# A recurrence with decaying weights: shared PSUM banks, sums tile by tile, k rounded by its load, quarter tiles, and an order written by a list schedule

## The chip, the cores and the metric

The kernel runs on one core of a Trainium2 chip. The metric is the device time of one execution in microseconds (us). A core has five engines that run side by side: PE (TensorE, the matrix engine, which writes into PSUM), DVE (VectorE), ACT (ScalarE), POOL (GpSimd) and SP (SyncE, used here to issue DMAs). Each has its own queue of instructions and works through it in the order in which the program was written; between engines, semaphores say when data is ready. DMAs are issued by SP and by POOL, and by ACT once. PSUM has eight banks of 512 f32 columns.

## The reference

For each of 16 batches and 256 channels a pair (aa, bb) runs through 2048 time steps; pp is the logarithm of a common scale that keeps the exponentials in range. All tensors are f32, k and v are 16 x 2048 x 256.

```
for t in range(seq_len):
    ww = u + k[t];  qq = max(pp, ww)
    e1, e2 = exp(pp - qq), exp(ww - qq)
    output[t] = (e1*aa + e2*v[t]) / (e1*bb + e2 + 1e-08)
    ww = pp - w + k[t];  qq = max(ww, k[t])
    e1, e2 = exp(ww - qq), exp(k[t] - qq)
    aa, bb, pp = e1*aa + e2*v[t], e1*bb + e2, qq
```

Without the scale this is: the output is (a + exp(u+k) v) / (b + exp(u+k)), and then a becomes exp(k-w) a + exp(k) v, and b becomes exp(k-w) b + exp(k). So the weight with which a step counts later is the exponential of a running sum of k and w.

## The kernel before

Time is cut into 16 chunks of 128 steps, a chunk into two halves of 64. A tile n holds chunk n // 4 and four batches: 128 partitions (steps) by 1024 columns (four batches by 256 channels, or two groups i of 512 columns). There are 64 tiles. Per tile:

- `load_k`, `load_v` (lines 61 to 69) bring k and v, 0.5 MB each. `round_k` (L166, DVE) copies k into a tile `km` of type float32r, which the f32 matmuls read.
- `logs` (L183, L187, PE) builds the exponents in the PSUM tile `X`, 128 x 2 x 2 x 512 f32, four banks: for each kind q (q = 0: weight in the running sum, q = 1: weight of the step's own output) and each column group one matmul with one or two rows (positions times w, and u), and one 128 x 128 matmul with k (the running sums inside a half).
- `exps` (L193, L195, ACT) writes their exponentials in bf16 to places 0 and 1 of the ring `EZR`, which has twelve tiles. The first `HALVES` = 9 tiles take their banks in turn from `X` and from the bank pair that later holds denominators, in two instructions; the later ones take one instruction for both kinds.
- `cast_v` (L199) makes v bf16 in `vb`, of which there is one buffer; on DVE for the first eleven tiles, then on POOL. `times_v` (L204, DVE) writes the products of places 0 and 1 with v to places 2 and 3.
- `den` (L321, PE) and `num` (L335, PE) multiply the triangular matrix `L` and the identity `Id` (scaled in `LN`, `IdN`) with places 0, 1 and 2, 3, four matmuls of 128 x 128 by 512 columns each. Both matrices are zero between the two halves of 64. `recip` (L327, L328, ACT) makes 1/den as exp(-ln(den)); `mult` (L340, DVE) writes num/den and L341 stores it on SP's queue.

The state between halves runs through a small chain, once per chunk: `sums` (L231, 32 matmuls over the chunk's four tiles, column by column of tiles), `copy_sums` (L239), `turn` (L246), `copy_turn` (L252), `state_logs` (L256, ACT), `state_shift` (L261, POOL), `state_frames` (L266, a scan on DVE), `state_offsets` (L270 to L274, POOL), `state_weights` (L277, ACT), `state_chain` (L281, L284, DVE), `state_spread` (L289), `turn_back` (L300, PE), and `inject` (L305 and four small DMAs, L310), which writes the incoming states over the last row of each half in `EZR`. Only then can the chunk's den and num run. The PSUM tiles of `sums`, `turn`, `turn_back` and `num` share one pair of banks (`psn`, tag `num`), and `den` has a pair of its own (`psd`).

The order is written by hand: one loop over slots n (line 370). In slot n the exponentials of tile n are taken, the logs of tile n+1, the denominators and numerators of tile n-10 (`LAG` = 10), and at fixed places the pieces of the chain for the chunk that ended one to four slots before, from the table at line 346. Loads up to tile 15 are issued by SP and later ones by POOL, each in the slot after which a buffer comes free (`NBUF` = 7 for k and for v).

Of the kernel before, what the change touches and what calls it, by code (L numbers as in the profile page):

```python
# [7 lines left out]
F32 = mybir.dt.float32  # L8
# [7 lines left out]
def kernel(  # L16
# [13 lines left out]
    HS = 64  # L30
# [6 lines left out]
    FIRST = 16  # L37
    HALVES = 9
    NBUF = 7
    RS = 2.0 ** -20  # L40
    CAP = 54.0
    BIG = 1e30

    consts = ctx.enter_context(tc.tile_pool(name="consts", bufs=1))
    kpool = ctx.enter_context(tc.tile_pool(name="kpool", bufs=NBUF))
    vpool = ctx.enter_context(tc.tile_pool(name="vpool", bufs=NBUF))
    vbpool = ctx.enter_context(tc.tile_pool(name="vbpool", bufs=1))
    rpool = ctx.enter_context(tc.tile_pool(name="rpool", bufs=2))
    opool = ctx.enter_context(tc.tile_pool(name="opool", bufs=3))
    small = ctx.enter_context(tc.tile_pool(name="small", bufs=2))  # L50
    psx = ctx.enter_context(tc.tile_pool(name="psx", bufs=1, space=bass.MemoryType.PSUM))
    psd = ctx.enter_context(tc.tile_pool(name="psd", bufs=1, space=bass.MemoryType.PSUM))
    psn = ctx.enter_context(tc.tile_pool(name="psn", bufs=1, space=bass.MemoryType.PSUM))

    kr_of, vr_of, VB = {}, {}, {}

    def rows_of(x, n):
        c, p = divmod(n, 4)
        return x[4 * p:4 * p + 4, c * TC:(c + 1) * TC, :].rearrange("n t d -> t n d")

    def load_k(n, q):
        kr = kpool.tile([128, 4, Dm], F32, tag="kr", name="kr")
        K(q.dma_start(out=kr, in_=rows_of(k, n)))  # L63
        kr_of[n] = kr

    def load_v(n, q):
        vr = vpool.tile([128, 4, Dm], F32, tag="vr", name="vr")
        K(q.dma_start(out=vr, in_=rows_of(v, n)))  # L68
        vr_of[n] = vr


    wuf = consts.tile([128, 2, Dm], F32, tag="wuf", name="wuf")

    def rows_wu(q, x, g0):
        q = K(q.dma_start(out=wuf[g0::32, :, :], in_=bass.AP(
            tensor=x.tensor, offset=x.offset, ap=[[0, (128 - g0 + 31) // 32], [0, 2], list(x.ap[0])])))

    rows_wu(SC, w, 0)
    load_k(0, SP)
    rows_wu(SP, u, 65)  # L80
    load_k(1, SP)
    for n in range(NBUF - 1):
        load_v(n, SP)
        if n + 2 < NBUF:
            load_k(n + 2, SP)
    K(SC.preload_act_table_set("natural_log_exp_and_others"))
    Z = consts.tile([128, D], BF16, tag="Z", name="Z")
    K(DVE.memset(Z, 0.0))
    M1 = consts.tile([128, 128], F32, tag="M1", name="M1")
    I1 = consts.tile([128, 128], F32, tag="I1", name="I1")  # L90
    K(DVE.memset(M1, -1.0))
    K(DVE.memset(I1, 0.0))
    idle = psn.tile([128, 2, D], F32, tag="num", name="idle")
    for j in range(10):
        K(PE.matmul(idle[:, j % 2, :], Z[:, 0:128], Z, start=True, stop=True, skip_group_check=True))
# [12 lines left out]

    select(M1, GE, 0.0, -1, -1, [[1, 128]])
# [7 lines left out]

# [6 lines left out]
    WU = consts.tile([128, D], F32R, tag="WU", name="WU")  # L124
    for g, r in ((0, 1), (32, 1), (64, 2), (96, 2)):
        K(DVE.tensor_copy(WU[g:g + r, :], wuf[g:g + r].rearrange("p n d -> p (n d)")))

    mats = {}

    def sum_matrices():  # L130
        OH = consts.tile([128, 56], BF16, tag="OH", name="OH")
        fill(OH, 0.0)
        for h in range(2):
            fill(OH[HS * h:HS * h + HS, 22 + h:23 + h], 1.0)
            fill(OH[HS * h:HS * h + 1, 30 + h:31 + h], 1.0)
        Sel = consts.tile([128, 3, 2, 2, 4, 2], F32, tag="Sel", name="Sel")
        fill(Sel, 0.0)
        for j, r in ((0, 64), (1, 0), (2, 8)):
            for h in range(2):
# [32 lines left out]
    def part_of(n, q):  # L172
        if n >= HALVES:
            return X[:, q]
# [264 lines left out]
```

## Time and profile before

| | |
|---|---|
| three runs | 367.5, 367.6, 369.11 us, median 367.6 |
| profiled execution, from first to last instruction | 365.5 us; its time outside the span is not given, the median lies 2.1 above |
| busy: PE, DVE, ACT, POOL | 304.1, 257.4, 257.6, 196.3 us |
| granted TensorE clock, mean | 0.844 |
| DMA | 101.52 MB, mean 278 GB/s |
| chain that ended last | PE 62%, DVE 20%, POOL 6%, ACT 5% |

The profile is one execution. "Busy" is the time in which at least one instruction of the engine ran; since matmuls are pipelined, a busy PE can hold shorter work than it shows, so PE is better read from one group's start to the next group's start. The granted clock is the share of the full TensorE clock that the chip allowed at that moment. The chain of waits is followed back from the last instruction: at each step to what released it, or to the instruction before it on the same engine. A group's line gives: line of the kernel, engine, operation, output and inputs, shapes, count, busy us and mean ns of one, and then the idle time of the engine just before and what ended it.

### The profile page before, as it was taken

Reading aid. Unit: us, or ns where it says so; the run is one execution under the profiler, and the core shown is the slowest. Engines: PE = TensorE matmul, PEld = TensorE weight load, DVE = VectorE, ACT = ScalarE, POOL = GpSimd, SP = SyncE. Lnnn points to the kernel's source line nnn. Section 1 sums busy time; section 2 is a strip of 40 time slices with the busy share of each in tenths; the row PEclk is TensorE's granted clock in tenths of the full one; section 3 lists DMA queues with packets and bytes.
Section 4 is the critical chain, followed back from the end, with each engine's and each line's share of the span. In section 5 each row is a group of like instructions: output and inputs, shape, how many; then the busy total and the mean of one; then the engine's idle time right before and its main releaser. Section 6 shows DMA issues by size and latency. Waiting matters only on the chain.

```text
span 365.5 us, 4884 instructions
## 1 busy us (share of the span) xinstructions
PE 304.1 (83%) x1674; PEld 143.6 (39%) x1674; DVE 257.4 (70%) x355; ACT 257.6 (70%) x234; POOL 196.3 (54%) x279
## 2 busy tenths in 40 slices
PE   7789797969799696987989697988969788976682
PEld 2335353535344243443435253444425343533230
DVE  4773867878857757588866887575686889883652
ACT  1553558879758677679768797576775789993782
POOL 2700457887837738477764677575465745250100
PEclk9556658999859679699958997695887999998997
DMA  7999998899998979989998999889797995242465
GB/s 222 354 348 348 351 341 254 281 372 300 355 314 246 316 238 319 298 255 318 336 318 256 344 315 352 284 275 296 257 317 244 324 308 177 77 159 95 143 223 179
DMA packets 67498, 101.52 MB, mean 278 GB/s; under 512 B 5894, under 2 KB 55186, under 8 KB 67474
## 3 DMA queue, kind: packets, MB, share of 16 engines
q0 software_dynamic: 14080, 50.40, 43.2%
q1 hardware_dynamic: 53382, 50.80, 42.2%
q8 instruction: 13, 0.21, 0.2%
q14 instruction: 11, 0.09, 0.1%
q10 hardware_dynamic: 12, 0.01, 0.0%
HBM read 67.12 MB, written 33.55 MB: 275 GB/s over the span
## 4 chain that ended last, share of the span: by engine, by line
PE 62%; DVE 20%; POOL 6%; ACT 5%; issue 3%; DMA 2%; SPq 0%; DVEq 0%; POOLq 0%; ACTq 0%
PE X L187 17%; PE num L335 15%; PE den L321 13%; PE X L183 7%; DVE ot L340 7%; PE tot L231 6%; DVE km L166 4%; DVE EZR L204 4%; ACT rd L327 3%; PE TS L246 2%; PE CT L300 2%; DVE AB L284 2%; DMA vr<-in_v_dram 2%; ACT EZR L193 2%; POOL U L271 2%
## 5 line engine op out<-in xcount | busy, mean ns | idle before, releaser
L195 ACT ACTIVATE EZR<-X 128x2048 bf16<-128x2048 f32 x55 | 102.7, 1868 | 32.3 <-PE X L187 32.3
L340 DVE TENSOR_TENSOR ot<-num,rd 128x1024 f32<-128x1024 f32 x64 | 78.2, 1222 | 30.5 <-ACT rd L327 10.5
L199 POOL CAST vb<-vr 128x1024 bf16<-128x1024 f32 x53 | 55.0, 1038 | 83.1 <-DVE EZR L204 83.1
L204 DVE TENSOR_TENSOR EZR<-EZR,vb 128x2048 bf16<-128x2048 bf16 x64 | 79.5, 1241 | 2.1 <-ACT EZR L193 1.9
L327 ACT ACTIVATE rd<-den 128x1024 f32<-128x1024 f32 x64 | 65.1, 1017 | 16.6 <-PE den L321 13.9
L328 ACT ACTIVATE rd<-rd 128x1024 f32<-128x1024 f32 x64 | 67.8, 1059 | 2.0
L321 PE MATMUL den<-EZR,L 128*128 128x512 bf16 x128 | 42.4, 416 | 22.6 <-ACT rd L327 22.2
L166 DVE CAST km<-kr 128x1024 fp32r<-128x1024 f32 x64 | 55.5, 867 | 2.4 <-PE X L187 1.9
L187 PE MATMUL X<-km,NLE 128*128 128x512 f32 x128 | 54.1, 508 | 1.8 <-DVE km L166 0.9
L183 PE MATMUL X<-WU,CO 1*128 1x512 f32 (+1 forms) x256 | 42.8, 563 | 10.0 <-ACT EZR L195 5.8
L335 PE MATMUL num<-EZR,LN 128*128 128x512 bf16 x128 | 41.9, 412 | 8.7 <-DVE cb L305 5.7
L187 PE MATMUL X<-km,NLZ 128*128 128x512 f32 x128 | 47.8, 459 | 0.0
L68 POOL DMA_DIRECT2D vr<-in_v_dram x48 | 40.0, 832 | 5.0 <-DVE vb L199 4.2
L321 PE MATMUL den<-EZR,Id 128*128 128x512 bf16 x128 | 41.4, 407 | 0.0
L335 PE MATMUL num<-EZR,IdN 128*128 128x512 bf16 x128 | 41.3, 406 | 0.0
L63 POOL DMA_DIRECT2D kr<-in_k_dram x48 | 39.9, 830 | 0.0
L183 PEld LDWEIGHTS X<-WU,CO 1*128 1x128 f32 (+1 forms) x256 | 15.9, 205 | 47.2 <-issue 16.6
L193 ACT ACTIVATE EZR<-X 128x1024 bf16<-128x1024 f32 x18 | 17.9, 1022 | 20.2 <-PE X L187 20.1
L187 PEld LDWEIGHTS X<-km,NLZ 128*128 128x128 f32 x128 | 27.1, 219 | 9.2 <-issue 3.4
L187 PEld LDWEIGHTS X<-km,NLE 128*128 128x128 f32 x128 | 22.0, 215 | 20.3 <-issue 16.1
L239 DVE COPY ts<-tot 128x256 f32<-128x256 f32 x16 | 6.8, 425 | 32.2 <-PE tot L231 32.2
L231 PE MATMUL tot<-EZR,OH 128*32 128x256 bf16 x512 | 25.3, 364 | 1.4 <-DVE ot L340 1.4
(60 smaller groups left out, 233.3 us busy)
## 6 DMA issues: line engine op xcount, KB each, us to landing
out_dram<-ot SPq DMA_DIRECT2D x64, 512.0 KB, 5.4
kr<-in_k_dram POOLq DMA_DIRECT2D x48, 512.0 KB, 6.2
vr<-in_v_dram POOLq DMA_DIRECT2D x48, 512.0 KB, 7.3
kr<-in_k_dram SPq DMA_DIRECT2D x16, 512.0 KB, 8.8
vr<-in_v_dram SPq DMA_DIRECT2D x16, 512.0 KB, 8.7
EZR<-cb SPq DMA_DIRECT2D x56, 8.0 KB, 4.6
EZR<-cb POOLq DMA_DIRECT2D x8, 8.0 KB, 5.0
wuf<-in_w_dram ACTq DMA_DIRECT2D x1, 8.0 KB
```

The source lines that it names most:

```text
L166: K(DVE.tensor_copy(km, kr_of.pop(n)))
L183: K(PE.matmul(part_of(n, q)[:, i, :], CO[g:g + 1 + q, :], WU[g:g + 1 + q, :], start=True, stop=False, tile_position=(g, 0), skip_group_che ...
L187: K(PE.matmul(part_of(n, q)[:, i, :], (NLE, NLZ)[q], km[:, i, :], start=False, stop=True, skip_group_check=True))
L195: K(SC.activation(ez(n)[:, 0:2], X, ACT.Exp))
L199: K(eng.tensor_copy(vb, vr_of.pop(n)))
L204: K(DVE.tensor_mul(ez(n)[:, 2:4], ez(n)[:, 0:2], vb.unsqueeze(1).broadcast_to([128, 2, 2, D])))
L231: K(PE.matmul(t[32 * j:32 * j + 32, :], mats["OH"][:, s:s + 32], ez(4 * c + p)[:, 2 * q, i, 256 * x:256 * x + 256], start=p == 0 and x == ...
L321: K(PE.matmul(d[:, i, :], mats[m], ez(n)[:, q, i, :], start=q == 0, stop=q == 1, skip_group_check=True))
L327: K(SC.activation(rd, DEN.pop(n), ACT.Ln, scale=RS))
L328: K(SC.activation(rd, rd, ACT.Exp, scale=-1.0))
L335: K(PE.matmul(d[:, i, :], mats[m], ez(n)[:, q, i, :], start=q == 2, stop=q == 3, skip_group_check=True))
L340: K(DVE.tensor_mul(o.rearrange("p (i n) d -> p i (n d)", i=2), NUM.pop(n), RD.pop(n)))
```

## The change

- k is loaded directly into float32r tiles by POOL's DMAs, from tile 4 on; for the first four tiles SP loads it and DVE rounds it (`round_k`). w and u are loaded as float32r too. Loads from tile 4 on are POOL's.
- `X` is now two pairs of banks, given out to whoever comes next: logs of kind 0, logs of kind 1, or denominators. Logs and exponentials are two steps per tile, one per kind. `num` keeps a pair, `sums` has one bank of its own, and `turn`, `turn_back` share one.
- `sums` runs after each tile (8 matmuls) instead of once per chunk (32).
- `den` and `num` use 64 x 64 matmuls, eight per tile and kind, each in a quarter of the array; for the second column group the two halves of 64 steps land swapped, and `store` writes the output with three DMAs: one for two batches, two for the swapped halves of the others.
- The small POOL operations of the chain move to DVE. `vb` has two buffers, k and v eight.
- The order comes from a list schedule run while the program is built: each step has an engine, an assumed cost, what it follows, a due time and a buffer that it takes and gives back; the step that can start first is written next, and among those of one engine within 0.2 us the one due first. The assumed time of a tile is 3.9 us, the rates of the loads 0.35 and later 0.40 MB per us.

```diff
-    psx = ... psd = ... psn = ...
+    psx, psn, pst, pss = ...
     def load_k(n):
+        if n < BYSP:
+            KR[n] = vpool.tile([128, 4, Dm], F32, tag="vr", name="kf")
+            K(SP.dma_start(out=KR[n], in_=rows_of(k, n)))
+        else:
+            KR[n] = kpool.tile([128, 4, Dm], F32R, tag="kr", name="kr")
+            K(POOL.dma_start(out=KR[n], in_=rows_of(k, n)))
...
+    def logs(n, q, a):
+        km = KR[n].rearrange("p (i n) d -> p i (n d)", i=2)
+        for i in range(2):
+            g = 32 * (2 * q + i)
+            K(PE.matmul(X[:, a, i, :], CO[g:g + 1 + q, :], WU[g:g + 1 + q].rearrange("p n d -> p (n d)"),
+                        start=True, stop=False, tile_position=(g, 0), skip_group_check=True))
+        for i in range(2):
+            K(PE.matmul(X[:, a, i, :], (NLE, NLZ)[q], km[:, i, :], start=False, stop=True, skip_group_check=True))
-            K(SC.activation(ez(n)[:, 0:2], X, ACT.Exp))
+    def exps(n, q, a):
+        K(SC.activation(ez(n)[:, q], X[:, a], ACT.Exp))
...
+    def sums(n):
+        c, p = divmod(n, 4)
...
-        K(POOL.tensor_tensor(U[:, FR, :, 1:3], U[:, L1, :, 0:2], U[:, L1, :, 1:3], ALU.add))
+        K(DVE.tensor_tensor(U[:, FR, :, 1:3], U[:, L1, :, 0:2], U[:, L1, :, 1:3], ALU.add))
...
-                K(PE.matmul(d[:, i, :], mats[m], ez(n)[:, q, i, :], start=q == 0, stop=q == 1,
-                            skip_group_check=True))
+    def apply(out_tile, n, names, q0):
+        for s in range(2):
+            for i in range(2):
+                for h in range(2):
+                    r, o = HS * h, HS * ((h + i) % 2)
+                    K(PE.matmul(out_tile[o:o + HS, i, :], mats[names[s]][r:r + HS, r:r + HS],
+                                ez(n)[r:r + HS, q0 + s, i, :], start=s == 0, stop=s == 1,
+                                tile_position=(r, o), skip_group_check=True))
+    def den(n, a):
+        apply(X[:, a], n, ("L", "Id"), 0)
+    def num(n):
+        NUM[n] = psn.tile([128, 2, D], F32, tag="num", name="num")
+        apply(NUM[n], n, ("LN", "IdN"), 2)
...
+    def store(n):
+        c, p = divmod(n, 4)
+        o = OT.pop(n)
+        K(SP.dma_start(out=out[4 * p:4 * p + 2, c * TC:(c + 1) * TC, :].rearrange("n t d -> t n d"), in_=o[:, 0:2, :]))
+        for h in range(2):
+            t0 = c * TC + HS * (1 - h)
+            K(SP.dma_start(out=out[4 * p + 2:4 * p + 4, t0:t0 + HS, :].rearrange("n t d -> t n d"),
+                           in_=o[HS * h:HS * h + HS, 2:4, :]))
...
-    for n in range(NP + LAG + 2):
...
+            step(("LK", n), q, qc, load_k, (n,), behind=[("LK", n - 1)], due=t - 14 * SLOT, take=("V", -1 - n) if early else ("K", n), move=0.524)
+            step(("X", j, n), "ACT", 0.94, exps, (n, j), [("L", j, n), ("NUM", n - RING), ("S", n - RING)],
+                 [("X", 1 - j, n - 1 + j)], t, give=[("X", (j, n))])
+        step(("DEN", n), "PE", 0.55, den, (n,), [("IN", c)], [("DEN", n - 1)], t + e, take=("X", ("d", n)))
+        step(("LN", n), "ACT", 0.95, log_den, (n,), [("DEN", n)], [("INV", n - 1)], t + e, take=("RD", n),
+             give=[("X", ("d", n))])
+        step(("ST", n), "SP", 1.6, store, (n,), [("MUL", n)], due=t + e + 4, move=0.524)
...
+        pick = []
+        for eng, some in best.items():
+            t0 = min(some, key=lambda x: x[0])[0]
+            pick.append(min((x for x in some if x[0] <= t0 + 0.2), key=lambda x: x[1]))
+        t, _, name = min(pick, key=lambda x: x[:2])
```

## The prediction

> **What bounds the kernel now.** I read the table by stage first. The stages are cut at the first exponential (9.10 us), at that of tile 16 (80.86) and at that of tile 63 (322.79); the fifth row is the end of the steady stage, the last one a short dense stretch. Columns: length, busy time of PE, PEld, DVE, ACT and POOL with their instructions, granted clock, DMA share, GB/s.
>
> ```profile
> 0.00:9.10 9.10, 6.91 (x20) 2.52 (x20) 4.07 (x14) 1.29 (x2) 1.87 (x10) 1.00 0.72 221
> 9.10:80.86 71.76, 61.96 (x292) 29.56 (x292) 51.99 (x81) 44.28 (x43) 38.36 (x63) 0.71 1.03 330
> 80.86:322.79 241.93, 209.13 (x1231) 100.76 (x1231) 180.14 (x236) 186.47 (x166) 151.21 (x198) 0.87 0.88 285
> 322.79:365.50 42.71, 26.12 (x135) 10.79 (x133) 21.23 (x27) 25.59 (x27) 4.84 (x10) 0.91 0.48 162
> 292.61:322.79 30.18, 27.05 (x191) 13.85 (x191) 26.12 (x36) 27.68 (x26) 12.34 (x18) 1.00 0.55 181
> 160.00:167.00 7.00, 4.40 (x21) 1.83 (x18) 5.80 (x9) 5.07 (x6) 6.24 (x10) 1.00 1.04 383
> ```
>
> In the steady stage 47 tiles take 241.93 us, 5.15 each, and no engine is full: PE 86%, at a granted clock of 0.87, ACT 77%, DVE 74%, DMA 0.88. In the fifth row, with the clock at 1.00 and the loads over, the same order needs 30.18/7 = 4.31 us. So about 0.84 us per tile is lost to the clock and the transfers. Where, the chain of waits shows (start, length, what):
>
> ```profile
> 181.08 1.20 POOL U L271
> 182.28 0.07 issue
> 182.36 0.44 POOL U L272
> 182.79 0.02 issue
> 182.82 0.37 ACT G L277
> 183.18 0.92 ACT rd L327
> 184.10 0.04 issue
> 184.14 1.88 PE den L321 x4
> 186.02 0.61 PE CT L300 x4
> 186.63 0.02 issue
> 186.66 0.30 DVE cb L305
> 186.96 0.04 issue
> 187.00 1.87 PE num L335 x4
> 188.87 0.73 PE X L183 x2
> 189.59 2.00 PE X L187 x4
> ```
>
> The small chain of each chunk stands in the fixed order: ACT waits for POOL before L277, then PE for ACT, and PE is idle from 182.58 to 184.14. Then the clock falls to 0.50 (until 193.6): four den matmuls take 1.88 us instead of 0.86, four L187 2.00 instead of 1.12. What the operations cost, in groups:
>
> ```profile
> L195 ACT ACTIVATE EZR<-X 128x2048 bf16<-128x2048 f32 x55 | 102.7, 1868 | 32.3 <-PE X L187 32.3
> L199 POOL CAST vb<-vr 128x1024 bf16<-128x1024 f32 x53 | 55.0, 1038 | 83.1 <-DVE EZR L204 83.1
> L166 DVE CAST km<-kr 128x1024 fp32r<-128x1024 f32 x64 | 55.5, 867 | 2.4 <-PE X L187 1.9
> ```
>
> **The change, part by part**, per tile at full clock unless said.
>
> *ACT.* The exponential over 2048 columns becomes two over 1024. Back to back, three such take 2.90 us, 0.967 each, so 1.93 against 1.75 (185.09 to the next start at 186.84). Ln and Exp of a denominator stay: 1.06 from start to start, then 0.96. The chain's two, 0.33 and 0.37, come once in four tiles: 0.17. Sum 4.13 (before 3.95). This is the new floor.
>
> *PE.* Before: const matmuls L183 0.44 to the next start, L187 0.57 and 0.46, den 0.86, num 0.88, sums 0.27, TS and CT 0.23: 3.71. The new den and num are eight 64x64 matmuls in four quadrants. No row shows quadrants. The nearest is L231, column tiles: 32 of 256 columns in 0.99 us (85.08 to 86.07), where one after another at den's 0.215 per 512 they would take 3.4. By it eight take 0.49; if only pairs overlap they take 0.86, one by one 1.72. I take 0.53 each, with one switch of shape: sums after L187 start 0.56 after its first matmul (84.52 to 85.08), den after L187 0.46 (88.91 to 89.37 for TS), so a switch costs 0.10. Each half of the logs: two const matmuls, between 0.22 and 0.44, take 0.33, plus 0.51 for two of L187: 1.68 for both. Sums of one tile 0.35, TS and CT 0.23. Sum 3.32.
>
> The Trainium skill, TensorEngine Tiling, Key Properties, says that changing the tiling mode drains the engine. The trace agrees (0.10 per switch). By it the four or so switches per tile that 3.32 doesn't hold add 0.4, PE comes to 3.7 and the gain on PE is gone, but ACT still binds at full clock.
>
> *DVE.* L166 goes for 60 of 64 tiles (0.867 each, of it up to 0.8 waiting when a POOL cast runs beside). Per chunk it takes over from POOL six small additions and copies of 64 columns: 128 columns cost 0.30 (L281), memsets of 128 columns 0.17, so 0.17 to 0.30, I take 0.23, 1.4 per chunk, 0.35 per tile. On the chain these replace POOL's 0.31, 0.66, 1.20 and 0.43. DVE is left with 1.24 + 1.22 + about 1.1 = 3.5: hidden.
>
> *POOL.* 120 loads instead of 96 at 0.83, the casts at 1.04: 2.70 per tile, hidden. With a second vb buffer the cast need not wait for L204 (83.1 us) but can run beside it. The chunk's L271 took 1.20 beside L204 and 0.34 alone, so a cast may be held up to 1.24: 3.94, still under ACT. The Trainium skill, SBUF — State Buffer, Who interferes with whom, says a VectorE instruction with two SBUF inputs contends with a GpSimd one that reads SBUF; the trace agrees, and by it the hold is paid, not avoided: 3.94 rather than 2.70, no change of the sum.
>
> *Queues.* SP has three stores per tile instead of one at about 0.4 to 0.5 each (0.37 at 183.25), and the injections (2.41 per chunk): some 2.1 per tile. An injection written behind a store waits for that tile's product on DVE, and the next four dens wait for it. POOL's loads wait for a free buffer, and what stands behind one (a cast) waits too, then L204.
>
> *DMA.* 1.57 MB per tile. While only SP loads, the rate is 348 GB/s; with POOL's loads 383 over 7 us (last row above). So 4.1 per tile at 383, 4.5 at 348. k now changes its type on the way. No row shows that. Below: no gain, the bytes are the same. Above: the packet price could grow; at one and a half times nothing much is left over, the point is in the second rival. I take the plain load, the same queue and size (6.2 us to landing).
>
> *Stages.* First exponential: stays at 9.1 (w and u now land rounded, which saves 1.75 of casts, but POOL issues before the masks). Six tiles without outputs go by reads: 1.05 MB at 348 is 3.0, with logs at half clock 3.3: 20. The other 57 go at s. Floor of s is 4.13 (ACT); the old order's best chunks between 80 and 210 took 18.8 us, 4.7 per tile, with transfers running. I take the middle, 4.4: 251. Tail from exponential 63: its times_v 1.3, sums 0.4, the chain (0.43, 0.5, 0.36, 0.33, 0.6, 0.6, 0.37, 1.0, 0.44, 0.4, 0.29 and some 1.5 of handovers) 6.8, injection and landing 5, the last four denominators 8.6, product 1.2, stores 5, the exponential itself 1.9: 30. Before this was 42.7 because the last chain ran slot by slot; the older six denominators (12.3 of ACT) cover the new chain.
>
> Sum: 9.1 + 20 + 251 + 30 = 310. The span before is 365.5, the median of the three runs 367.6 (367.5 to 369.11), so 2.1 are added: 312.
>
> **Rivals.**
>
> *PE stays the bound* (**344**). Quadrants overlap only in pairs (den and num 0.86 each) and the clock stays at the 0.87 of before: 3.98/0.87 = 4.57 plus 0.4 of handovers is 4.97. 9.1 + 20 + 57 x 4.97 + 31 + 2 = 345, rounded to 344. For it: two bank pairs serve three uses per tile, so PE and ACT must alternate; the clock was 0.50 in all of 10 to 32 us with PE waiting between short groups. Against: L231 overlaps 3.5 to 1, and the idle stretch of 1.5 us per chunk is what the change removes. The drain rule above would give 3.7/0.87 = 4.25 plus 0.4, 4.65: about 326, inside this case.
>
> *The converting load is slow* (**400**, slower). All bytes at 400 GB/s (single microseconds reach 395 to 435) need 254 us, with start and tail 282. k is 31.5 MB through POOL, 79 us of that. If its packets cost 2.5 times the plain ones, 118 are added: 400. It decides from about 2.1 times (85 us more than 282 is 367). For it: the DMA share is already 0.88 to 1.04, no cover is left. Against: queue 0 moves 4 KB packets and 43.2% of the span for 50.40 MB is the same price as queue 1's 42.2% for 50.80.
>
> *Everything at the floor* (**295**): s = 4.13, 9.1 + 20 + 235 + 28 + 2. DMA would have to hold 381 GB/s throughout; 160 to 167 us shows it can for 7 us.
>
> *The order doesn't hold* (**367**): it is fixed beforehand from assumed durations; where loads or products come later, the engines wait in other places. With s = 5.15 as before the start and the tail still give 355; at s = 5.37 all is gone. For it: the assumed 0.94 for an exponential and 0.55 for den have no slack. Against: eight buffers of k and v, and the old fixed order had its long waits at one known place.
>
> **How the numbers follow.** Forecast (300 to 327) 0.48; floor 0.10; PE bound (327 to 363) 0.23; slow loads 0.13, one-by-one quadrants (PE 5.7, over 390) 0.03; the order not holding 0.03, most of it within 0.5%. A difference under 0.5% (1.8 us) can't be told from none here. Faster: 0.48 + 0.10 + 0.23 = 0.81; same 0.02; slower 0.17. The range 294 to 367 leaves out the lower part of the floor case and the slow loads and quadrants, 2 in 10.
>
> **What would show it.** Right: ACT above 90% in the steady stage, granted clock near 1.00, chain of waits led by ACT, L166 in four instances only, the tail near 30 us, k landing in about 6 us. Wrong: den groups of over 0.9 us at full clock; k landing much later than v, DMA share at 1.0 with GB/s under 300; ACT waiting for PE in every tile at a clock below 0.9; SP's injections issued several us after their copy.

## The result and the profile after

The changed kernel takes 556.34 us (median of four runs, 555.05 to 557.26). The kernel before, run beside it, takes 368.36 us. The ratio is 1.509, interval 1.499 to 1.519. I had forecast 312 us and a range up to 367. The sign was wrong, and none of my cases, not even the slow loads at 400, came near.

The stages of the changed kernel are cut at the first exponential (9.01 us), at 90 us and 30 us before the end (524 us). The columns are those of the table of before: length, busy time of PE, PEld, DVE, ACT and POOL, granted clock, DMA share, GB/s.

```profile
9.01:90.00 80.99, 59.15 (x216) 24.76 (x216) 26.94 (x48) 28.90 (x32) 25.33 (x45) 0.50 0.88 232
90.00:524.00 434.00, 346.12 (x1807) 141.00 (x1807) 184.38 (x292) 216.49 (x236) 123.69 (x142) 0.51 0.65 172
524.00:554.00 30.00, 15.41 (x148) 5.82 (x147) 15.30 (x22) 20.02 (x21) 0.00 (x0) 0.68 0.70 196
```

In the steady stage PE is busy 80%, ACT 50%, DVE 42%, the DMA share is 0.65, and the granted clock is 0.51. Nothing is full, and the clock is at half nearly all the time. The kernel before had 0.87 there with PE at 86%. In 350 us from 100 us on there are 84 exponentials, so a tile takes 350/42 = 8.33 us where it took 5.15. The tail, from the start of the last exponential (515.69 us) to the end, is 38.3 us where I had 30. What the operations cost, in groups:

```profile
L172 ACT ACTIVATE EZR<-X 128x1024 bf16<-128x1024 f32 x128 | 124.9, 1021 | 191.6 <-PE X L169 189.8
L83 POOL DMA_DIRECT2D kr<-in_k_dram x60 | 45.6, 760 | 281.9 <-PE X L169 281.9
L300 PE MATMUL X<-EZR,L 64*64 64x512 bf16 x256 | 40.4, 608 | 75.2 <-ACT EZR L172 71.9
L176 POOL CAST vb<-vr 128x1024 bf16<-128x1024 f32 x54 | 58.1, 1076 | 52.5 <-DVE EZR L181 52.4
```

ACT's exponentials wait 189.8 us for the logs, and the denominators' matmuls wait 71.9 us for the exponentials. Each of the two waits for the other. POOL's k loads wait 281.9 us for a k buffer that the logs free; this follows from PE, and is no cause. The DVE casts of k are gone but for the first four tiles, as the change says, and the wait of POOL's casts for DVE's products fell from 83.1 to 52.4 us.

The chain of waits over one tile (start, length, what) shows the two engines' turns:

```profile
255.35 0.03 ACT EZR L172
255.38 0.90 issue
256.27 1.03 ACT EZR L172
257.30 0.04 issue
257.34 1.09 PE X L300 x8
258.44 0.02 issue
258.46 1.03 ACT rd L309
259.49 0.04 issue
259.54 0.79 PE X L166 x2
260.33 1.15 PE X L169 x2
261.48 0.72 PE X L166 x2
262.20 1.17 PE X L169 x2
263.37 0.02 issue
263.39 0.03 ACT EZR L172
```

One round is 263.39 - 255.35 = 8.04 us, and it is a plain sum: both logs on PE 3.83, both exponentials on ACT 1.95 (the 0.90 of "issue" is the first of the two, which the chain passes over), denominators on PE 1.12, logarithm on ACT 1.08. On this chain PE and ACT never overlap; the inverse and, in this round, the numerators run beside it (in the round before, eight numerator matmuls stand on it between the two logs, 1.00 us; the mean of 8.33 holds such rounds too). The first exponential starts only when the logs of *both* kinds are done, although they lie in different banks, and the next tile's logs wait for the logarithm of the denominators, which uses one of the two pairs. This is not what a kernel with two independent pairs does. In the code, `X` is one PSUM tile of four banks. The order of the pieces fits waits that are made for a tile as a whole, so that two pairs of banks inside one tile hand over as one; the first experiment tests this.

That is the first theory: **turns**, from the one tile. The second is the **clock**: at 0.50 a piece on PE lasts up to twice as long. Whether the clock follows from the turns (PE waits) or from the shapes of the matmuls was open.

### The profile page after: what moved, and what is told of

The parts are those of the page before. It is cut to its first block, busy times and chain, and to the rows that moved or that the text cites. A ratio compares the mean times of both kernels' runs of the same rounds, so it can differ in the third digit from the quotient of the medians.

```text
span 554.0 us, 6016 instructions
## 1 busy us (share of the span) xinstructions
PE 427.4 (77%) x2186; PEld 173.9 (31%) x2186; DVE 231.5 (42%) x384; ACT 266.7 (48%) x289; POOL 156.5 (28%) x204
## 3 DMA queue, kind: packets, MB, share of 16 engines
q0 software_dynamic: 40416, 62.93, 43.6%
## 4 chain that ended last, share of the span: by engine, by line
PE 62%; ACT 27%; issue 6%; DMA 2%; DVE 2%; SPq 0%; DVEq 0%; ACTq 0%; POOLq 0%
PE X L169 27%; ACT EZR L172 18%; PE X L166 17%; PE X L300 11%; ACT rd L309 8%; PE num L300 5%; PE TS L223 3%; DVE ot L321 1%; DMA WU<-in_w_dram 1%; DMA out_dram<-ot 1%; ACT rd L313 0%; SPq L330 0%; PE tot L210 0%; PE CT L274 0%; SPq L327 0%
## 5 line engine op out<-in xcount | busy, mean ns | idle before, releaser
L172 ACT ACTIVATE EZR<-X 128x1024 bf16<-128x1024 f32 x128 | 124.9, 1021 | 191.6 <-PE X L169 189.8
L166 PE MATMUL X<-WU,CO 1*128 1x512 f32 (+1 forms) x256 | 100.5, 781 | 37.6 <-ACT EZR L172 20.5
L83 POOL DMA_DIRECT2D kr<-in_k_dram x60 | 45.6, 760 | 281.9 <-PE X L169 281.9
L309 ACT ACTIVATE rd<-X 128x1024 f32<-128x1024 f32 x64 | 65.5, 1023 | 81.5 <-PE X L300 50.6
L300 PE MATMUL X<-EZR,L 64*64 64x512 bf16 x256 | 40.4, 608 | 75.2 <-ACT EZR L172 71.9
L169 PE MATMUL X<-kr,NLZ 128*128 128x512 f32 x128 | 77.7, 708 | 0.0
L169 PE MATMUL X<-kr,NLE 128*128 128x512 f32 x128 | 77.2, 704 | 0.0
L166 PEld LDWEIGHTS X<-WU,CO 1*128 1x128 f32 (+1 forms) x256 | 36.2, 280 | 120.6 <-ACT rd L309 47.0
L176 POOL CAST vb<-vr 128x1024 bf16<-128x1024 f32 x54 | 58.1, 1076 | 52.5 <-DVE EZR L181 52.4
L300 PE MATMUL num<-EZR,LN 64*64 64x512 bf16 x256 | 41.3, 606 | 6.8 <-DVE ot L321 6.8
L300 PE MATMUL X<-EZR,Id 64*64 64x512 bf16 x256 | 42.8, 611 | 0.0
L300 PE MATMUL num<-EZR,IdN 64*64 64x512 bf16 x256 | 41.8, 611 | 0.0
L169 PEld LDWEIGHTS X<-kr,NLZ 128*128 128x128 f32 x128 | 31.9, 309 | 27.7 <-issue 27.7
L169 PEld LDWEIGHTS X<-kr,NLE 128*128 128x128 f32 x128 | 31.7, 308 | 27.6 <-issue 25.2
```

The costliest lines, as they stand in the source:

```text
L83: K(POOL.dma_start(out=KR[n], in_=rows_of(k, n)))
L166: K(PE.matmul(X[:, a, i, :], CO[g:g + 1 + q, :], WU[g:g + 1 + q].rearrange("p n d -> p (n d)"), start=True, stop=False, tile_position=(g, ...
L169: K(PE.matmul(X[:, a, i, :], (NLE, NLZ)[q], km[:, i, :], start=False, stop=True, skip_group_check=True))
L172: K(SC.activation(ez(n)[:, q], X[:, a], ACT.Exp))
L176: K((DVE if n < EARLY else POOL).tensor_copy(vb, VR.pop(n)))
L300: K(PE.matmul(out_tile[o:o + HS, i, :], mats[names[s]][r:r + HS, r:r + HS], ez(n)[r:r + HS, q0 + s, i, :], start=s == 0, stop=s == 1, tile ...
```

## The experiments

**Two tiles.** The two pairs become two PSUM tiles; nothing else changes, and the order is the same.

```
-    X = psx.tile([128, 2, 2, D], F32, tag="X", name="X")
+    X = [psx.tile([128, 2, D], F32, tag=f"X{j}", name=f"X{j}") for j in range(2)]
...
-        K(SC.activation(ez(n)[:, q], X[:, a], ACT.Exp))
+        K(SC.activation(ez(n)[:, q], X[a], ACT.Exp))
```

> One edit to the changed kernel: the PSUM tile X of two bank pairs becomes two tiles of one pair each; order, steps and work stay. Theory A: the program waits by tile, so with one tile each exponential waits for all logs written before it and each den for all exponentials, PE and ACT take turns, PE has idle stretches of 1.5 to 2 us in each tile and stays at half clock. Then this edit alone brings 300 to 340 us, a mean granted clock above 0.85 and exponentials of kind 0 under the logs of kind 1. Rival B: the many short matmuls in quarters, strips and single rows keep the clock low whatever the waits: clock near 0.52, time above 450. Rival C: the converting load of k is the bound: time above 500 with DMA share near 1.

Measured: 348.18, 358.31, 371.31 and 387.29 us, median 364.81, against 372.3 before. The granted clocks were 0.773, 0.751, 0.719 and 0.666 in the same order. That is neither forecast: the time is above the 300 to 340 us and the clock under the 0.85 of theory A, but far from the 450 us of rival B. The turns themselves are gone, as three rows of its trace at half clock show: the exponential of kind 0 starts while the logs of kind 1 run.

```profile
262.14 0.79 PE L166 MATMUL X<-WU,CO 2*128 2x512 f32 x2
262.86 1.22 PE L169 MATMUL X<-kr,NLZ 128*128 128x512 f32 x2
262.25 1.02 ACT L172 ACTIVATE EZR<-X 128x1024 bf16<-128x1024 f32 x1 [0.60 <-DMA out_dram<-ot]
```

With the turns went some 190 us, but the time now depends on how long the clock stays low. The trace of its slowest execution (387.29 us) has the clock at full and at half, in the table of stretches (columns as above):

```profile
150.00:170.00 20.00, 18.16 (x162) 8.40 (x162) 17.22 (x27) 18.18 (x23) 12.54 (x16) 1.00 1.16 339
180.00:200.00 20.00, 20.00 (x102) 7.77 (x102) 10.78 (x20) 12.41 (x14) 7.62 (x9) 0.50 1.00 301
210.00:250.00 40.00, 35.92 (x320) 15.46 (x316) 34.11 (x59) 37.07 (x44) 25.28 (x30) 1.00 1.19 357
255.00:315.00 60.00, 60.00 (x315) 22.82 (x314) 32.95 (x47) 38.13 (x42) 23.13 (x27) 0.50 0.91 253
```

At full clock ACT is busy 93%, and 20 exponentials fall in 40 us: 4.0 us per tile, somewhat below my floor. From 255 to 315 us PE has no gap, and yet the clock is 0.50; a tile then takes 6.3 us. So waits of PE do not explain the low clock there. It has a cause of its own.

**PE kept busy.** The changed kernel, with 18 more matmuls per tile whose weights are zero, so that they add nothing to the sums; X stays one tile.

```
+        for j in range(18):
+            K(PE.matmul(t, Z[:, 0:128], ez(n)[:, 0, j % 2, 0:256], start=False, stop=False, skip_group_check=True))
```

> The changed kernel with X as one tile, plus 18 matmuls per tile with zero weights (128x128 by 256 columns, 1.9 us at full clock) into the sums' bank, right before the den that waits for the exponentials; results don't change. It fills PE's idle stretch. If the half clock is most of the loss (and follows from the idle stretch): clock above 0.9, a tile of 1.9 (logs) + 2.3 (sums and filling, beside the exponentials) + 0.5 (den) + 1.1 (Ln) = 5.8 us, in all 390 to 430 us although PE has more to do. If the turns alone are the loss and the clock matters little: 540 to 570. If the shapes keep the clock low (rival B): clock 0.5 and 560 to 690 us.

Measured: 486.12 us (one run) at a clock of 0.893; the time lies between the forecasts. PE was given more work and the kernel became 70 us faster. The full-array matmuls raised the clock, and they replaced idle PE time; part of them lies on the path, so the run prices neither cause alone.

**Quarters undone, alone and with two tiles.** The denominators and numerators are again four matmuls of 128 x 128, with one store.

```
-                for h in range(2):
-                    r, o = HS * h, HS * ((h + i) % 2)
-                    K(PE.matmul(out_tile[o:o + HS, i, :], mats[names[s]][r:r + HS, r:r + HS], ...
+                K(PE.matmul(out_tile[:, i, :], mats[names[s]], ez(n)[:, q0 + s, i, :], ...
```

> Two tiles as in the first run, and den and num again as four matmuls of 128x128 each, with one store per tile as before the change. If ACT is the floor once the turns are gone: within 3% of the first run. If PE binds: 0.67 us per tile more on PE at full clock, 20 to 45 us above the first run. If quarters of the array lower the granted clock: faster than the first run, at a higher clock.

> The changed kernel with X as one tile, and only the quarters undone: den and num as four matmuls of 128x128, one store per tile. If the shape of the matmuls alone decides the clock: clock above 0.85, a tile of 1.9 (logs) + 1.9 (exponentials) + 0.9 (den) + 1.1 (Ln) + small = 6.0 us, 400 to 440 us. If the idle stretches of the turns hold the clock down too: clock 0.50 to 0.60, den longer on the path, 560 to 620 us.

Measured with two tiles: 336.91 us (335.78 to 338.0), ratio 0.906 (0.900 to 0.912), at a clock of 0.92. This was the first version of which every run was faster than the kernel before. Its table of stretches:

```profile
10.00:56.00 46.00, 45.78 (x152) 19.59 (x153) 19.97 (x32) 23.17 (x25) 21.57 (x40) 0.50 1.36 342
100.00:250.00 150.00, 146.18 (x848) 64.42 (x863) 122.37 (x182) 132.96 (x146) 88.20 (x102) 1.00 1.16 349
```

While there are no denominators, up to 56 us, the clock is at 0.50 here too, with PE busy all the time. Only the logs run there (with the sums), so the cause lies at least partly in them. Once the full-array denominators and numerators run too, the clock is 1.00 (100 to 250 us).

Measured with one tile: 543.64 us (541.29 and 546.0), ratio 1.470 (1.455 to 1.485), clocks 0.70 and 0.78, between the two forecasts. Undoing the quarters alone buys 13 us: the first theory stands, the turns are the larger loss, and they don't need the low clock. In a stretch of this run at a clock of 0.98, three tiles still take 20 us.

**Quarters put into the kernel before.** The same `apply` and three stores in the kernel before, with its order unchanged.

> The kernel before with one part of the change: den and num in quarters and the three stores, in the old order with the old banks. If quarters lower the granted clock: clock below 0.75 (before: 0.82 to 0.89 in these runs) and 390 to 480 us. If they only shorten PE's work: clock as before, 345 to 368 us.

Measured: 368.2 us (367.0 to 369.41), ratio 0.996 (0.992 to 0.9999). PE's busy time fell from 304.1 to 281.9 us, and the clock from 0.84 to 0.72. So each forecast was half right: the clock fell, and the time stayed. That the clock takes back what the quarters save fits these numbers; no run here tests it alone. It pointed at the quarters as the cause of the low clock.

**The clock by shape.** Ahead of the kernel before, streams of bf16 matmuls of one shape each, all with 512 columns to stream, write to banks that are not yet in use; ACT work makes a pause between the streams. They add work and leave nothing out.

```
+    for j, (kind, reps) in enumerate((("full", 14), ("quarter", 28), ("rows", 28), ("cols", 28), ("strips", 28), ("one", 28), ("full", 14))):
...
+            elif kind == "one":
+                yield bench[:, i, :], M[64 * i:64 * i + 1, :], RB[64 * i:64 * i + 1, i, :], dict(tile_position=(64 * i, 0))
```

> The kernel before with a stretch ahead of it, which computes nothing that is used: streams of bf16 matmuls of 512 columns back to back, 6 to 12 us each, with 8 us of PE idle between: full 128x128; quarters 64x64, four at a time; 64x128 (rows halved); 128x64 (columns halved); strips 128x32; single rows 1x128; full again. If quarters don't count as activity for the clock: full goes from 0.50 to 1.00 inside its stretch, quarters stay at 0.50 throughout; the others tell whether rows or columns are what counts. If any back-to-back stream raises the clock: all reach 1.00 within 4 to 7 us.

The pauses came out at 1.0 to 2.7 us, so most streams inherited the clock of the stream ahead: quarters, half-arrays of 64 rows and column strips held 1.00 for 6.2 us each. One row of the table of stretches tells something new: the single-row stream (62.87 to 75 us), and the full arrays behind it.

```profile
62.87:68.87 6.00, 6.00 (x31) 0.50 0.00 0
68.87:74.87 6.00, 6.00 (x30) 0.50 0.00 0
74.87:78.60 3.73, 3.73 (x12) 0.50 0.00 0
78.60:82.20 3.60, 3.60 (x17) 0.93 0.02 5
```

(Columns: length, PE busy with its instructions, clock, DMA share, GB/s.) PE is full for 12 us with matmuls of one row, and the clock stays at 0.50. The full arrays behind them (from 75.0 us) raise it at 79.1 us.

**The clock from cold.** As before, with a pause of some 11 us before each stream, and three mixtures in the proportions of a tile: all shapes, without the single rows, and with full arrays for quarters.

```
+    tile_of = (("one", 1), ("full", 1), ("one", 1), ("full", 1), ("strips", 1), ("quarter", 4))
+    streams = ([("quarter", 36)], [("rows", 36)], [("cols", 36)], [("strips", 36)],
+               tile_of * 3, tuple(x for x in tile_of if x[0] != "one") * 4, (tile_of[:5] + (("full", 4),)) * 3)
```

> The kernel before with a stretch ahead of it whose products are not used: seven streams of bf16 matmuls of 512 columns, each after some 10 us in which PE is idle, so that each starts at half clock. In order: quarters (64x64, four at a time), rows halved (64x128), columns halved (128x64), strips (128x32), 15 us each; then what PE does for one tile, repeated back to back, in three mixtures: single rows, full, single rows, full, strips, quarters (as in the two-tile run with quarters); the same without the single rows; and the first with full arrays in place of the quarters. If quarters as such can't raise the clock: stream 1 and the first two mixtures stay at 0.50, the third reaches 1.00. If it is the single rows, whose own stream stayed at 0.50 for 12 us in the run before: streams 1 to 4 reach 1.00, the first mixture stays at 0.50 or takes longest, the second reaches 1.00.

```profile
19.73:25.60 5.87, 5.87 (x57) 0.50 1.07 338
25.60:30.40 4.80, 4.80 (x92) 1.00 0.05 15
104.40:110.90 6.50, 6.50 (x33) 0.50 0.01 3
110.90:115.00 4.10, 4.10 (x34) 1.00 0.00 0
127.39:131.40 4.01, 4.01 (x25) 0.50 0.00 0
131.40:138.00 6.60, 6.60 (x72) 1.00 0.01 2
```

The first two rows are quarters alone: the clock reaches 1.00 after 5.9 us. So quarters can raise it. The mixture with single rows (rows three and four) takes 6.5 us, without them (the last two) 4.0, and with full arrays for the quarters 5.7. These times don't rank the mixtures. In every trace of this case the clock is 0.50 or 1.00 and each stretch of it, up to the cut at the end, lasts a whole number of 3.413 us. In this run 5.9, 6.5, 4.0 and 5.7 us are each what was left of the running 3.413 us when the stream began (2.4, 3.1, 0.6 and 2.3 us), plus one whole. So all four raised the clock at the end of their first whole one, the mixture with single rows too, though I had expected it to stay low or to take longest for its rows. Only single rows alone, in the run before, never raised it, through two whole ones. The theory that I took from it: matmuls of one or two rows, L166, keep PE busy but don't count for the clock. In the two-tile kernel at half clock they take 4 x 0.36 = 1.44 of 6.3 us per tile (23%); with full arrays the numerators and denominators add some 1.4 at half clock, and it is 1.44 of 7.7 (19%). Quarters would then only do their harm by making the rest shorter. The mixture in this run doesn't reproduce the kernel's low clock: its single rows took 1.08 of the 5.41 us of its first tile (20%), it is bf16 where the kernel's logs are f32, and it rose. So the theory rests on the next runs.

**Single rows made full.** w, u and the position weights get 128 rows, of which all but one or two are zero; the sums are the same. Three kernels: two tiles with quarters, two tiles with full arrays, and the changed kernel with one tile.

```
+    fill(WU, 0.0)
...
-            g = 32 * (2 * q + i)
-            K(PE.matmul(X[a][:, i, :], CO[g:g + 1 + q, :], WU[g:g + 1 + q].rearrange("p n d -> p (n d)"),
-                        start=True, stop=False, tile_position=(g, 0), skip_group_check=True))
+            K(PE.matmul(X[a][:, i, :], CO[:, q, :], WU.rearrange("p n d -> p (n d)"),
+                        start=True, stop=False, skip_group_check=True))
```

> Two tiles for X, quarters kept, and the w and u matmuls written over all 128 rows: their rows but one (or two) are zero, so the sums are the same. PE's work per tile is then 4 x 0.43 of logs and the rest as before. If the single-row matmuls, which alone held the clock at 0.50 for 12 us, are what keeps it down where PE is back to back, the clock of the profiled run rises above 0.9, no 20 us stretch with PE busy stays at 0.50, and the time falls from 365 us to 315 to 340 us. If the quarters keep the clock down (or the sum of small matmuls of any kind), the clock stays at 0.6 to 0.78 and the time at 345 to 390 us.

> Two tiles for X, full-array denominators and numerators, one store, and the w and u matmuls over all 128 rows. If the change from single rows to the full array costs PE some 0.2 us in each half (a half takes 1.08 us where four matmuls of 0.215 us are 0.86), PE loses 0.4 us per tile and the time falls from 337 us to 318 to 332 us, where the exponentials, the logarithms and the transfers are next. If not, the half stays at 1.08 us or the order is the limit, and the time stays within 333 to 345 us.

> The changed kernel with one edit: the w and u matmuls over all 128 rows. X stays one tile, so PE and ACT still take turns. If the single rows are what holds the clock down, the clock rises from 0.52 above 0.85 although PE waits for ACT in every tile, and at 6 us a tile the time is 390 to 440 us. If the waiting of PE holds it down too, the clock stays under 0.75 and the time is 480 to 560 us.

Measured: 315.25 us (315.17 to 315.81), ratio 0.852 (0.847 to 0.858), with quarters; 317.55 us (316.68 to 318.85), ratio 0.859 (0.851 to 0.866), with full arrays; 480.27 us for the changed kernel with one tile. The clocks are 0.944, 0.979 and 0.829. The first came as the theory said. In it, the spread of 39 us that the single rows had is down to 0.6. Its PE clock in 40 slices of the span, and the end-to-end chain's shares, from its page:

```profile
PEclk9799979997999997999999988979999999999955
...
DMA 46%; DVE 19%; ACT 11%; PE 9%; issue 5%; SPq 4%; POOL 4%; DVEq 0%; POOLq 0%
```

The clock is up, and PE has 9% of the chain: transfers bound this version, at 367 GB/s and a DMA share of 1.20 from 50 to 250 us. In that stretch 89 exponentials make 4.49 us per tile. One thing went otherwise than expected. In the second kernel I had counted on a cheaper half of the logs; it hardly did (1.01 us at full clock with full rows, 0.99 and 1.09 with single rows). The gain there is the clock, from 0.92 to 0.98, mostly in the start. The third kernel met neither forecast: its clock rose to 0.83, but the time is above the 390 to 440 us that I gave for that. Its trace holds the turns at full clock (251.81 to 257.73 us, clock 1.00): one round is 5.92 us, again a plain sum, of 2.15 for the logs, 1.95 for the exponentials, 0.67 for the denominators and 1.07 for the logarithm, with handovers. From 100 to 400 us a tile takes 6.90 us, at a mean clock of 0.85.

The two causes, with the two-tile median of the first experiment in the last corner:

| | single rows | full rows |
|---|---|---|
| one tile | 556 | 480 (one run) |
| two tiles | 365 (348 to 387) | 315 |

The one tile costs 165 to 191 us by the medians, the single rows 50 to 76. Against the fastest two-tile run with single rows (348.18) the pairs are 208 and 33, since that corner moves with its clock.

**Rows in use or change of tiling.** A full matmul also ends a change of tiling between L166 and L169. So two more kernels keep two tiles, quarters, and two matmuls side by side as with the single rows, with 32 rows each and with 64.

```
-            K(PE.matmul(X[a][:, i, :], CO[g:g + 1 + q, :], WU[g:g + 1 + q].rearrange("p n d -> p (n d)"),
+            K(PE.matmul(X[a][:, i, :], CO[g:g + 32, :], WU[g:g + 32].rearrange("p n d -> p (n d)"),
```

> Two tiles for X, quarters kept, and the w and u matmuls over strips of 32 rows in the places that the single rows had, so that they run two at a time and PE changes its tiling as before. If what counts is how many rows a matmul has, the clock of the profiled run is above that of the single rows (0.67 to 0.77 there), at 0.85 or more, and the time 315 to 340 us. If what held the clock down were the changes of tiling or two strips side by side, the clock stays at 0.78 or less and the time at 345 to 390 us.

> Two tiles for X, quarters kept, and the w and u matmuls over halves of 64 rows, two side by side as with the single rows and the strips of 32, so that PE changes its tiling as before, while all 128 rows are in use. If the rows in use are what counts (32 a matmul, 64 at a time, left the clock at 0.74), the clock of the profiled run is above 0.88 and the time is 312 to 335 us. If the change of tiling, or two side by side, is what holds it down, the clock stays at 0.78 or less and the time at 345 to 390 us.

Measured: with 32 rows 345.01 to 369.85 us, median 358.41, at clocks of 0.72 to 0.81, nearly as with one row, and inside the forecast of the rival; with 64 rows 324.77 us (323.21 to 326.73), ratio 0.875 (0.867 to 0.883), at clocks of 0.88 to 0.94. The clock in 40 slices, with 32 rows and with 64:

```profile
PEclk9555555555596598958789999995555999999785
```

```profile
PEclk9555597699999999598799999999999999999575
```

In all three kernels two matmuls run side by side and the tiling changes between them and the full ones, and with 64 rows the clock rises: so neither the change nor the pairing holds it down. The rows in use fit: 32 a matmul are too few in this mixture. One rival is left. The single rows and the 32 rows are placed at strips of 32 (tile_position 0, 32, 64, 96), the 64 rows at halves (0, 64), so these runs can't tell the number of rows from the size of the strip; 32 rows, four at a time, were not tried. Nor are 64 rows as good as 128: the start of the 64-row kernel still has five slices at 0.5, which 128 rows don't.

**Full rows in the kernel before.**

> The kernel before with one edit: its w and u matmuls over all 128 rows. Its profiled run had a clock of 0.82, with stretches at half. If the single rows are what cost it those stretches, the clock rises above 0.93 and the time falls to 335 to 358 us. If its own order and waits set the time (it has one tile for the logs too, taken whole by one exponential), the clock may rise but the time stays within 360 to 370 us.

Measured: 350.54 us (346.95 to 351.03), ratio 0.948 (0.941 to 0.956), clock 0.964 where the kernel before has 0.84. The kernel before paid for its single rows as well. Against it on these terms the mended change (315.25) is 10% faster.

**What k's rounding by the load is worth.** k is loaded as it is and rounded on DVE for all tiles, with seven buffers each for the loads of k and v (eight in the changed kernel) and two for the rounded k; once with two tiles and quarters, once with two tiles and full arrays. A third kernel rounds on POOL from tile 10 on.

```
-            KR[n] = kpool.tile([128, 4, Dm], F32R, tag="kr", name="kr")
-            K(POOL.dma_start(out=KR[n], in_=rows_of(k, n)))
+        KR[n] = kfpool.tile([128, 4, Dm], F32, tag="kf", name="kf")
+        K((SP if n < BYSP else POOL).dma_start(out=KR[n], in_=rows_of(k, n)))
```

> Two tiles as in the first run, but k loaded as f32 (seven buffers for k and seven for v, as before the change) and rounded on DVE for all 64 tiles. If the converting load costs nothing: equal to the first run or up to 20 us slower, from 0.69 us more on DVE per tile. If its four times as many packets (40416 on POOL's queue where before there were 14080) cost transfer time: 10 us or more faster than the first run, with a lower DMA share for the same bytes.

> Two tiles and full-array den and num (third run of the first set), with k loaded as f32 and rounded on DVE. That run moved some 350 GB/s at a DMA share of 1.16 in its steady stage, where before POOL's plain loads reached 383 at 1.04. If the converting load's packets (1 KB instead of 4 KB) set the pace there: 5 to 20 us faster than that run. If PE sets it: within 2%. If DVE's 0.69 us more per tile and its waits set it: 5 to 30 us slower.

> Two tiles and full arrays, k loaded as f32 in 4 KB packets and rounded on POOL from tile 10 on (DVE before). If the plain packets' higher rate (383 GB/s before, 350 with converting loads) is worth something once DVE has no rounding to do: 320 to 335 us. If the rounding's place in the order is what costs (rounding on DVE took 378): 345 to 380 us.

Measured: 412.78 us (404.09 to 420.32), ratio 1.093 (1.081 to 1.106); 378.76 us (368.42 to 405.38), ratio 1.005 (0.997 to 1.013); 415.22 us (414.36 to 418.87), ratio 1.123 (1.115 to 1.132). Against the same kernels with the converting load (365 and 337) the first two are 48 and 42 us slower by the medians, and 56 and 33 from fastest run to fastest. All three are slower than any of my forecasts; for the third, what sets its time was not sought. The longest waits in the second kernel are not for transfers but for DVE and the buffers behind it:

```profile
POOL vb L173 <- DVE EZR L178: 71.6, 40, 6.1
POOL kf L80 <- DVE kr L156: 68.7, 32, 6.7
```

(What waits, for what: us in total, times, longest.) So the converting load isn't what slows the kernel. Without it, rounding on DVE with these buffers costs 33 us or more in this order; the rounding and the fewer buffers were not taken apart, and with full rows, where transfers bind, the plain load was not tried. The converting load costs packets: 40416 instead of 14080 on its queue, for 62.93 MB and 50.40 MB.

**Costs of the planner.** The version with two tiles and full arrays, its schedule built from durations of the trace.

```
-    SLOT = 3.9
+    SLOT = 4.5
...
-            step(("L", j, n), "PE", 0.8, logs, ...
+            step(("L", j, n), "PE", 1.08, logs, ...
-        step(("DEN", n), "PE", 0.55, den, ...
+        step(("DEN", n), "PE", 0.88, den, ...
```

> Two tiles and full arrays (the 337 us run), with the list schedule's assumed costs set to what the trace shows: logs 1.08 per half, exponential 0.97, den and num 0.88, Ln 1.03, its exponential 1.00, sums 0.40, a tile 4.5, loads 0.35 MB per us throughout. If the assumed costs matter for the order: 5 to 15 us faster than that run. If transfers and PE set the pace anyway: within 1%.

Measured: 357.26 us (351.3 to 366.38), ratio 0.952 (0.943 to 0.962), clock 0.886: 20 us slower by the medians than with the wrong costs, 13 between the nearest runs, and a miss. The order matters by more than I allowed for, and better costs did not make it better. Which step of the new order does it was not tried.

## Why the prediction was wrong

**The step that failed** is the sum under *ACT* and *PE*: I set a tile at the floor of one engine (4.13, taken as 4.4), as if the two pairs of banks were given out independently. The program gives out one tile, and a round is a sum over both engines, not a maximum. By rows of the trace at half clock, the sum is 3.83 + 1.95 + 1.12 + 1.08 = 8.0. It fails at full clock too: with one tile and full rows a round was 5.92 us. The mean tile of 8.33 instead of 4.4, 57 times, is 224 of the 244 us between forecast and result. My own text held the sentence for it, "two bank pairs serve three uses per tile, so PE and ACT must alternate", and I used it only in the rival *PE stays the bound*, priced at 0.4 of handovers. The place to look was one line of the diff, where `X` is still a single tile.

**The second fault** is the clock. I expected it "near 1.00"; the rival took 0.87. It was 0.51. I read the clock of before (0.71 in the start, 0.50 in all of 10 to 32 us) as a result of PE waiting. It came mostly from the single-row matmuls: with full rows, and nothing else changed, the kernel before has 0.96.

Of the other steps:

- *ACT.* 1.93 forecast for the two exponentials of a tile, 1.95 measured in the round above. The size was right; what was missing is that PE's pieces add to it.
- *Quadrants.* Right: four at a time. At full clock in the two-tile kernel a denominator group is followed by the next group 0.43 to 0.56 after its start, a numerator group 0.55 (forecast 0.53). Neither pairs nor one by one.
- *Logs.* 1.68 forecast for both halves, 2.19 measured at full clock (1.09 and 1.10). Two single-row matmuls take 0.43 to the next start, as four did before; I had let them go down to 0.33. The two start 2 or 3 ns apart, side by side, and yet the full matmul behind them starts 0.43 later, while in the kernel with full rows one matmul follows the other after 0.22 to 0.24. So about 0.2 of the 0.43 (an estimate from these rows) goes with the change of tiling, twice the 0.10 that I had read. This fits the drain that the Trainium skill, TensorEngine Tiling (Array Packing), Key Properties, describes. It also explains why full rows, with no change inside the half, made it no shorter: 1.01 (full arrays) to 1.13 (quarters), since two full matmuls in a row take about as long as the pair with its change.
- *Sums, TS and CT, DVE, POOL.* 0.35 forecast for the sums, 0.34 measured at full clock; DVE and POOL stayed hidden in the changed kernel (2% and 0% of its chain).
- *DMA.* k lands in 4.7 us in the changed kernel and v in 5.3, at 172 GB/s: the rival *The converting load is slow* is not the cause. At 4.49 us per tile (two tiles, full rows) the rate is 367 GB/s and transfers bound, between my ends of 383 and 348; k then lands in 13.2 us and v in 13.9.
- *The whole sum.* With both faults mended the kernel takes 315 us where I had 312, near by luck as far as its bound goes: I had ACT as the floor, and transfers bound it. That the numbers are near does not make the forecast right, since the kernel that was to be forecast has both faults. The tail there is 36.5 us from the last exponential's start (277.2 to 313.7), against 30.
- *The rivals.* The sum of *PE stays the bound* comes to 345, and I wrote 344; nothing hangs on it. I gave the slower side to slow loads, quadrants one by one and a failing order. The cause was none of them.

Of what I listed as signs of being wrong, one was there: "ACT waiting for PE in every tile at a clock below 0.9".

**What stays open.** The four runs of the changed kernel have mean clocks of 0.524, 0.526, 0.589 and 0.718 and yet times within 0.4%, while in the two-tile kernel time follows the clock. The Trainium skill, TensorE: Matmul & The Clock Gate, Seeing it yourself, warns that recorded clock events on trn2 have been seen to be unreliable; in the one trace of the changed kernel, the pieces of PE do last 1.7 to 1.8 times as long as in the two-tile kernel at full clock (1.15 against 0.66 us for two of L169, 0.81 against 0.46 for a denominator group), so there the 0.5 is real. For the other three runs I can't tell. So what the clock costs the changed kernel I take from the kernel with full rows (76 us, one run, whose clock is still 0.83), not from the record. Open too is why the mixture of shapes ahead of the kernel before reached 1.00 with its single rows, while the two-tile kernel stays at 0.50 for 60 us.

## What to carry to other kernels

When a buffer is to be split between uses, split it into tiles: here the program waited for the tile, and a pair of banks inside a shared tile bought nothing. If each of two engines is half busy and each waits for the other in every round, add the pieces of one round from the chain; if the sum is the period, look for the shared object before looking at any engine's speed. And if the clock stays at half while PE is back to back, look for matmuls with few rows, and pad them with zeros: here that was worth 18 us in the kernel before, and 33 to 72 us in the changed kernel with two tiles.

## What was not expected of the hardware

- Matmuls of one row, back to back for 12 us, leave the clock at 0.50, and in the mixture of the two-tile kernel 32 rows do little better (0.72 to 0.81 against 0.67 to 0.77); 64 rows bring 0.88 to 0.94, 128 rows 0.94. The Trainium skill, TensorE: Matmul & The Clock Gate, What's actually happening, says the clock follows how busy PE has lately been, in a window of some 3.4 us. The traces agree on the window: the clock stays the same for whole numbers of 3.413 us, and the streams of full, half and quarter arrays have 1.00 after 3.3 to 5.9 us, at the end of the first whole one or, for the 3.3, of one that had just begun. The single rows do not agree, since PE was busy throughout.
- Padding a matmul from 1 row to 128 with zeros cost PE almost nothing, since the change of tiling goes with it: a half of the logs took 1.01 us at full clock instead of 0.99 to 1.09 with full arrays around it, and 1.13 instead of 1.09 with quarters.
- A load that rounds f32 on the way splits into more packets (40416 against 14080 on that queue) and keeps 349 to 367 GB/s with a DMA share of 1.16 to 1.20.
